# Row means of a 64 MB array: the first load issued as two transfers from two engines

## The chip, the cores and the metric

The kernel runs on one core of a Trainium2 chip. The time is device microseconds of one execution; of three runs of the kernel before, the median is 160.81 us (160.39 to 160.96). The profile is of one execution, taken apart into its engines: DVE (VectorE) and ACT (ScalarE) compute here, POOL (GpSimd) does two small multiplications, SP (SyncE) issues every DMA, and PE (TensorE) does nothing. The data is moved by the core's 16 DMA engines. A DMA is issued by a queue (SP's, in the kernel before), cut into one packet for each of the 128 partitions, and the packets are dealt out to the 16 DMA engines, eight to each.

## The reference

```python
batch, seq, dim = 32, 512, 1024
x = np.random.randn(batch, seq, dim).astype(np.float32)
divisor = float(dim)

def reference(x, divisor):
    return (np.sum(x, axis=-1) / divisor).astype(np.float32)
```

16,384 rows of 1,024 float32 values, 67.1 MB, are read once; 16,384 means, 64 KB, are written.

## The kernel before

The rows are spread over 128 partitions, 128 rows to each. The rows of one load that belong to one partition lie side by side in memory, so a load of n rows is 128 pieces of n x 4 KB. The loads come in this order, by rows per partition: 2 and 14 (list `first`), six of 14 and one of 12 (list `main`), then 9, 4 and 2 (list `last`), and the last row in two halves, `pa` and `pb`. All the loads are issued by SP in program order, one after the other, on one DMA queue (`load`, L182).

The loads of 14 rows, and the first one of 2 rows, go to three buffers in turn (pool `bulk`). So the first three loads (2, 14 and 14 rows) need to wait for nothing. The fourth goes to the buffer of the first, and SP issues it when DVE's reduction of the first load is done; the fifth waits for the reduction of the second, and so on. The tile framework gives each DMA one of eight completion semaphores in turn.

DVE sums most rows with one `reduce_sum` for each load (L205, tile names `res<-t`); from the load numbered eight on, ACT takes some of the rows (L186, `junk<-t`), and for the last 16 rows DVE uses another instruction (L192). POOL multiplies by 1/1024 (L207). Two stores of results are issued by SP during the end of the stream (L223, L224), and the last one, 8 KB, after the last sum (L228).

Three functions rewrite the program after it is built. `start_loads_at_once` takes the DMAs that stand at the head of SP's instructions and wait for nothing (here the first three loads) and puts them ahead of SP's part in the opening barrier, in which all engines meet before the kernel's body. `latest_wait_first` sorts the waits of an instruction that has several. `close_while_storing` puts the last store within the closing barrier. An instruction that has more waits than it can hold gets a small semaphore instruction ahead of it.

Of the kernel before, what the change touches and what calls it, by code (L numbers as in the profile page):

```python
# [13 lines left out]
SP = mybir.EngineType.SP  # L14
DVE = mybir.EngineType.DVE
POOL = mybir.EngineType.Pool


def start_loads_at_once(nc):

    first, body = nc.main_func.blocks[0], nc.main_func.blocks[1]
    loads = []
    for i in body.instructions:
        if i.engine == SP:
            if type(i).__name__ != "InstDMACopy" or (i.sync_info and i.sync_info.on_wait):
                break
            loads.append(i)
    names = {i.name for i in loads}  # L30
    assert names
    body.instructions = [i for i in body.instructions if i.name not in names]
    at = next(
        k for k, i in enumerate(first.instructions) if i.engine == SP and type(i).__name__ == "InstDrain"
    )
    first.instructions = first.instructions[:at] + loads + first.instructions[at:]


def with_sync(i, on_wait=None, on_update=None):
# [29 lines left out]
def close_while_storing(nc, landed):  # L69
# [29 lines left out]
    def first(engine, among):  # L99
        i = next(i for i in among if i.engine == engine)  # L100
        assert type(i).__name__ == "InstDrain"
        return i

    enter, gather = first(SP, rest), first(POOL, rest)
    last = nc.sync.wait_ge(landed, 17).ins
# [20 lines left out]
@with_exitstack  # L126
def kernel(
    ctx: ExitStack,
    tc: tile.TileContext,
    x: bass.AP,  # L130
    divisor: float,
    out: bass.AP,
):
    nc = tc.nc
    landed = nc.alloc_semaphore("landed")
    nc.at_finalize(start_loads_at_once)
    nc.at_finalize(latest_wait_first)
    nc.at_finalize(lambda nc: close_while_storing(nc, landed))
    xf = x.flatten_outer_dims()
    N, D = xf.shape  # L140
    P = nc.NUM_PARTITIONS
    scale = 1.0 / float(divisor)
    J = N // P
    assert J * P == N


    F, L = 16, 16
    M = J - F - L
    W = M + L
    x_first = bass.AP(tensor=x.tensor, offset=0, ap=[[F * D, P], [D, F], [1, D]])  # L150
    x_main = bass.AP(tensor=x.tensor, offset=P * F * D, ap=[[W * D, P], [D, M], [1, D]])
    x_last = bass.AP(tensor=x.tensor, offset=P * F * D + M * D, ap=[[W * D, P], [D, L], [1, D]])
    o_first = bass.AP(tensor=out.tensor, offset=0, ap=[[F, P], [1, F]])
    o_main = bass.AP(tensor=out.tensor, offset=P * F, ap=[[W, P], [1, M]])
    o_last = bass.AP(tensor=out.tensor, offset=P * F + M, ap=[[W, P], [1, L]])


    first = [(2, 0), (14, 0)]
    main = [(14, 0)] * 5 + [(14, 4), (12, 5)]
    last = [(9, 4), (4, 2), (2, 1)]  # L160
    assert sum(n for n, _ in first) == F
    assert sum(n for n, _ in main) == M and sum(n for n, _ in last) == L - 1

    pad = ctx.enter_context(tc.tile_pool(name="pad", bufs=1))
    pad.tile([P, 224], F32, name="pad")
    bulk = ctx.enter_context(tc.tile_pool(name="bulk", bufs=3))
    one = ctx.enter_context(tc.tile_pool(name="one", bufs=1))
    psum = ctx.enter_context(tc.tile_pool(name="junk", bufs=4, space=bass.MemoryType.PSUM))


    c = 512
    t4 = one.tile([P, 4, D], F32, name="t4")
    t2 = one.tile([P, 2, D], F32, name="t2")
    pa = one.tile([P, 768], F32, name="pa")[:, :c]
    pb = one.tile([P, D - c + 16], F32, name="pb")[:, : D - c + 2]
    res0 = one.tile([P, F], F32, name="res0")
    res = one.tile([P, M], F32, name="res")
    fin = one.tile([P, L], F32, name="fin")
    nc.gpsimd.memset(pb[:, D - c :], 0.0)  # L179

    def load(dst, src):
        tc.keep_in_program_order(nc.sync.dma_start(out=dst, in_=src))  # L182

    def act_sum(dst, src, by=1.0):
        junk = psum.tile([P, D], F32, name="junk")
        nc.scalar.activation(junk, src, COPY, scale=by, accum_out=dst)  # L186

    def dve_mean(dst, src, by=scale):


        h = src.shape[-1] // 2
        nc.vector.tensor_tensor_reduce(  # L192
            out=src[:, :h], in0=src[:, :h], in1=src[:, h:], scale=by, scalar=0.0,
            op0=ADD, op1=ADD, accum_out=dst,
        )

    for loads, src, dst in ((first, x_first, res0), (main, x_main, res)):
        j = 0
        for rows, on_act in loads:
            t = bulk.tile([P, 14, D], F32, name="t")  # L200
            load(t[:, :rows, :], src[:, j : j + rows, :])
            d = rows - on_act
            for i in range(d, rows):
                act_sum(dst[:, j + i : j + i + 1], t[:, i, :])
            nc.vector.reduce_sum(out=dst[:, j : j + d], in_=t[:, :d, :], axis=AX)  # L205
            j += rows
        nc.gpsimd.tensor_scalar_mul(out=dst, in0=dst, scalar1=scale)  # L207
    j = 0
    for rows, on_act in last:
        t = bulk.tile([P, 14, D], F32, name="t")[:, :rows, :] if rows > 4 else t4 if rows == 4 else t2  # L210
        load(t, x_last[:, j : j + rows, :])
        d = rows - on_act
        for i in range(rows):
            if i < d:
                dve_mean(fin[:, j + i : j + i + 1], t[:, i, :])
            else:
                act_sum(fin[:, j + i : j + i + 1], t[:, i, :], by=scale)
        j += rows
    load(pa, x_last[:, j, :c])
    load(pb[:, : D - c], x_last[:, j, c:])  # L220


    tc.keep_in_program_order(nc.sync.dma_start(out=o_first, in_=res0))  # L223
    tc.keep_in_program_order(nc.sync.dma_start(out=o_main, in_=res))  # L224

    dve_mean(pb[:, D - c : D - c + 1], pa, by=1.0)
    dve_mean(fin[:, j:], pb)
    tc.keep_in_program_order(nc.sync.dma_start(out=o_last, in_=fin))  # L228
# [35 lines left out]
```

## Time and profile before

| what | value |
|---|---|
| median of three runs | 160.81 us (160.39 to 160.96) |
| span of the profiled execution, first to last instruction | 159.0 us |
| what lies around the span, by the median | 1.81 us |
| DVE busy | 117.2 us (74%) |
| ACT busy | 18.5 us (12%) |
| POOL busy | 1.0 us (1%) |
| DMA packets, bytes | 2448, 67.18 MB |
| rate over the span | 422 GB/s |
| time that packets took, of 16 engines' span | 98.3% |

The page lists no total for the profiled execution other than its span, so what the other runs have beyond it, 1.81 us, is taken as lying around it. Engines that are idle cost nothing unless the chain that ends last goes through them. A DMA packet is put down to the window in which it starts, so a share in a narrow window may be over 1 and in the next under it; wide windows even this out. "SPq" is SP's queue of issues. In a row of the timeline the number before the engine is the duration, and the bracket at the end tells how long the engine was idle and what ended this.

### The profile page before, as it was taken

What the parts mean: (1) busy time and instruction counts of PE and PEld (TensorE: products, weight loads), DVE (VectorE), ACT (ScalarE), POOL (GpSimd) and SP (SyncE); (2) the same over time, 40 slices, a digit from 0 to 9 for tenths busy, and PEclk for the clock granted to TensorE, in tenths of its full rate; (3) what the DMA queues carried; (4) which work ended last, traced back from release to release, by engine and by line L of the source; (5) the groups of instructions that cost most, each with busy time, mean ns of one, the idle gap of its engine ahead of it and who ended that gap; (6) DMA issues with size and microseconds to landing.
All of it is one profiled execution on the core that took longest, in us unless ns stands there. A gap on an engine that the chain in (4) does not pass through costs nothing.

```text
span 159.0 us, 148 instructions
## 1 busy us (share of the span) xinstructions
DVE 117.2 (74%) x29; ACT 18.5 (12%) x33; POOL 1.0 (1%) x7
## 2 busy tenths in 40 slices
DVE  0500059995999599978999599959995996395643
ACT  3000000000000000000000000000000900390684
POOL 0000000000000000000000000000000000001000
DMA  7999999959999999699999999699999999999894
GB/s 278 447 462 462 462 462 462 462 260 433 462 462 462 462 462 462 303 390 462 462 462 462 462 462 404 303 447 462 462 462 429 396 396 408 482 445 445 350 420 169
DMA packets 2448, 67.18 MB, mean 422 GB/s; under 512 B 656, under 2 KB 656, under 8 KB 912
## 3 DMA queue, kind: packets, MB, share of 16 engines
q1 hardware_dynamic: 2448, 67.18, 98.3%
HBM read 67.11 MB, written 0.07 MB: 422 GB/s over the span
## 4 chain that ended last, share of the span: by engine, by line
DMA 77%; DVE 21%; SPq 1%; issue 0%; DVEq 0%
DMA t<-in_x_dram 56%; DMA pb<-in_x_dram 21%; DVE res L205 20%; SPq L182 1%; DVE pb L192 0%; DVEq L259 0%
## 5 line engine op out<-in xcount | busy, mean ns | idle before, releaser
L205 DVE TENSOR_REDUCE res<-t 128x14 f32<-128x14336 f32 (+3 forms) x9 | 111.2, 12360 | 34.0 <-DMA t<-in_x_dram 34.0
L186 ACT ACTIVATE junk<-t 128x1024 f32<-128x1024 f32 x16 | 16.2, 1013 | 136.8 <-DMA t<-in_x_dram 136.8
L192 DVE CUSTOM_DVE_ANT_0 t<-t 128x512 f32<-128x512 f32 x8 | 5.1, 688 | 6.1 <-DMA t<-in_x_dram 6.1
L186 ACT ACTIVATION_READ_ACCUMULATOR junk<-t 128x1 f32 x16 | 3.0, 186 | 0.0
L207 POOL TENSOR_SCALAR res<-res 128x16 f32<-128x16 f32 (+1 forms) x2 | 0.7, 352 | 143.3 <-DVE res L205 143.3
L186 ACT ACT_TABLE_LOAD x1 | 1.3, 1283 | 1.7 <-PEq L245 1.7
L192 DVE DVE_READ_ACCUMULATOR2_ANT fin<- 128x1 f32 x9 | 0.7, 82 | 0.0
L192 DVE CUSTOM_DVE_ANT_0 pb<-pb 128x257 f32<-128x257 f32 x1 | 0.4, 428 | 0.2 <-DMA pb<-in_x_dram 0.2
L192 DVE CUSTOM_DVE_ANT_0 pa<-pa 128x256 f32<-128x256 f32 x1 | 0.4, 426 | 0.0
L179 POOL MEMSET pb<- 128x2 f32 x1 | 0.1, 99 | 1.3 <-POOLq L245 1.3
L245 POOL MEMSET const-bfloat16-1.0<- 128x1 bf16 x1 | 0.1, 101 | 0.0
L245 POOL MEMSET const-uint8-127<- 128x1 uint8 x1 | 0.1, 101 | 0.0
L245 POOL MEMSET const-float32-0.0<- 128x1 f32 x1 | 0.1, 98 | 0.2 <-issue 0.2
L245 POOL MEMSET const-float32-1.0<- 128x1 f32 x1 | 0.1, 98 | 0.0
L192 DVE DVE_READ_ACCUMULATOR2_ANT pb<- 128x1 f32 x1 | 0.1, 84 | 0.0
## 6 DMA issues: line engine op xcount, KB each, us to landing
t<-in_x_dram SPq DMA_DIRECT2D x7, 7168.0 KB, 35.6
t<-in_x_dram SPq DMA_DIRECT2D x1, 6144.0 KB, 33.3
t<-in_x_dram SPq DMA_DIRECT2D x1, 4608.0 KB, 27.2
t<-in_x_dram SPq DMA_DIRECT2D x2, 1024.0 KB, 19.2
t<-in_x_dram SPq DMA_DIRECT2D x1, 2048.0 KB, 31.7
pa<-in_x_dram SPq DMA_DIRECT2D x1, 256.0 KB, 33.8
pb<-in_x_dram SPq DMA_DIRECT2D x1, 256.0 KB, 33.9
out_dram<-res SPq DMA_DIRECT2D x1, 48.0 KB, 11.6
```

The costliest lines, as they stand in the source:

```text
L179: nc.gpsimd.memset(pb[:, D - c :], 0.0)
L182: tc.keep_in_program_order(nc.sync.dma_start(out=dst, in_=src))
L186: nc.scalar.activation(junk, src, COPY, scale=by, accum_out=dst)
L192: nc.vector.tensor_tensor_reduce(out=src[:, :h], in0=src[:, :h], in1=src[:, h:], scale=by, scalar=0.0, op0=ADD, op1=ADD, accum_out=dst,)
L205: nc.vector.reduce_sum(out=dst[:, j : j + d], in_=t[:, :d, :], axis=AX)
L207: nc.gpsimd.tensor_scalar_mul(out=dst, in0=dst, scalar1=scale)
L245: nc = _bacc.Bacc("TRN2", target_bir_lowering=False, num_devices=1)
```

## The change

The first load of two rows per partition becomes two DMAs of one row per partition. SP issues the first row, ACT the second. The function that moves loads ahead of the opening barrier does so now for SP and for ACT. The buffer, the computation, and every other load are as they were. The first reduction on DVE, and the load that later takes the buffer, each wait for both DMAs. Completion semaphores are handed out in turn, so each later load has the next one of the eight.

```diff
-    loads = []
-    for i in body.instructions:
-        if i.engine == SP:
-            if type(i).__name__ != "InstDMACopy" or (i.sync_info and i.sync_info.on_wait):
-                break
-            loads.append(i)
-    names = {i.name for i in loads}
-    assert names
-    body.instructions = [i for i in body.instructions if i.name not in names]
-    at = next(
-        k for k, i in enumerate(first.instructions) if i.engine == SP and type(i).__name__ == "InstDrain"
-    )
-    first.instructions = first.instructions[:at] + loads + first.instructions[at:]
+    for engine in (SP, ACT):
+        loads = []
+        for i in body.instructions:
+            if i.engine == engine:
+                if type(i).__name__ != "InstDMACopy" or (i.sync_info and i.sync_info.on_wait):
+                    break
+                loads.append(i)
+        names = {i.name for i in loads}
+        assert names
+        body.instructions = [i for i in body.instructions if i.name not in names]
+        at = next(
+            k
+            for k, i in enumerate(first.instructions)
+            if i.engine == engine and type(i).__name__ == "InstDrain"
+        )
+        first.instructions = first.instructions[:at] + loads + first.instructions[at:]
...
             t = bulk.tile([P, 14, D], F32, name="t")
-            load(t[:, :rows, :], src[:, j : j + rows, :])
+            if rows == 2:
+                load(t[:, 0, :], src[:, 0, :])
+                tc.keep_in_program_order(nc.scalar.dma_start(out=t[:, 1, :], in_=src[:, 1, :]))
+            else:
+                load(t[:, :rows, :], src[:, j : j + rows, :])
```

The two-row load in the list `last` is made by other lines and stays one DMA.

## The prediction, made before the changed kernel ran

> **What bounds the kernel now.** I read the table of windows first, for when the DMA engines are idle; then the chain that ended last, for what stands at its ends; then the timeline around the first loads, for the slack between the transfers and DVE; last, the end.
>
> The windows (columns: from, to, length, busy time of DVE, ACT and POOL with instruction counts, PE clock, DMA share, GB/s):
>
> ```profile
> 0.00:1.00 1.00, 0.00 (x0) 0.00 (x0) 0.19 (x4) 1.00 0.00 0
> 1.00:2.00 1.00, 0.00 (x0) 0.26 (x1) 0.10 (x1) 1.00 0.95 197
> 2.00:4.00 2.00, 0.00 (x0) 1.02 (x1) 0.00 (x0) 1.00 1.07 455
> 4.00:21.00 17.00, 2.29 (x1) 0.00 (x0) 0.00 (x0) 1.00 1.00 435
> 21.00:123.00 102.00, 90.52 (x6) 0.00 (x0) 0.26 (x1) 1.00 1.01 438
> ...
> 155.00:157.00 2.00, 1.07 (x4) 1.70 (x4) 0.00 (x0) 1.00 0.93 336
> 157.00:159.00 2.00, 0.43 (x2) 0.01 (x1) 0.00 (x0) 1.00 0.05 4
> ```
>
> Nothing moves in the first microsecond; in the second the engines are occupied (0.95) but at less than half the later rate; from 2 us on the share is about 1 until 155. So the kernel is one stream of 67.1 MB on 16 DMA engines that never run dry, with a start of about 2 us and a tail of about 2 us. DVE is busy 90.52 of 102 us in the middle, so it waits for the stream and not the stream for it.
>
> The chain that ended last, in order of time:
>
> ```profile
> 0.00 4.61 DMA t<-in_x_dram
> 4.61 0.02 issue
> 4.63 2.30 DVE res L205
> 6.93 0.02 issue
> 6.95 48.45 DMA t<-in_x_dram
> ```
>
> It goes through the first load, the first reduction and the fourth load's issue. That looks as if the first load's landing were on the path. It is not: the 48.45 us from 6.95 are mostly the fourth load standing in the queue behind loads two and three, as the timeline shows:
>
> ```profile
> 4.63 2.29 DVE L205 TENSOR_REDUCE res<-t 128x2 f32<-128x2048 f32 x1 [4.63 <-DMA t<-in_x_dram]
> 21.51 15.09 DVE L205 TENSOR_REDUCE res<-t 128x14 f32<-128x14336 f32 x1 [14.59 <-DMA t<-in_x_dram]
> 38.44 15.09 DVE L205 TENSOR_REDUCE res<-t 128x14 f32<-128x14336 f32 x1 [1.84 <-DMA t<-in_x_dram]
> 55.42 15.09 DVE L205 TENSOR_REDUCE res<-t 128x14 f32<-128x14336 f32 x1 [1.89 <-DMA t<-in_x_dram]
> ```
>
> Loads of 14 rows land at 21.5, 38.4 and 55.4, 16.93 to 16.98 us apart; DVE needs 15.09 for one and idles 1.8 to 1.9 before each. The fourth load, issued at 6.95, is first served when the third is nearly in, about 38. Its issue has some 30 us to spare. After the first reduction DVE idles 14.59 us.
>
> The end, from the timeline:
>
> ```profile
> 153.37 1.03 ACT L186 ACTIVATE junk<-t 128x1024 f32<-128x1024 f32 x1 [0.61 <-DMA t<-in_x_dram]
> 155.86 1.03 ACT L186 ACTIVATE junk<-t 128x1024 f32<-128x1024 f32 x1 [0.30 <-DMA t<-in_x_dram]
> 157.10 0.43 DVE L192 CUSTOM_DVE_ANT_0 pb<-pb 128x257 f32<-128x257 f32 x1 [0.17 <-DMA pb<-in_x_dram]
> 157.56 0.33 SPq L228 DMA_DIRECT2D out_dram<-fin  x1
> ```
>
> The last half row lands, DVE adds it, the last store is issued, and 1.4 us later it has landed. The end moves only if the stream ends earlier or later.
>
> **The change, part by part.** The sum is made on the profiled span, 159.0; the 1.81 us between it and the median is kept as it is, since no row shows it.
>
> SP's first issue. It covers the same 128 partitions with pieces of 4 KB instead of 8. SP's issue rows are 0.33 to 0.48 us long, whether a packet has 57 KB or 64 bytes, so halving bytes doesn't shorten it (the first one's row is 0.38). Loads two and three follow at 0.43 and 0.91 as before. Cost 0.
>
> ACT's issue. By the trace, ACT reaches its drain in the opening barrier at 0.13 us, SP at 1.40 behind its three issues, and the barrier opens at about 1.67. One issue of up to 0.48 brings ACT there at about 0.6: hidden behind SP's. If ACT needed over 1.4 us, the barrier would open later; behind it are ACT's table load (1.28 us, needed at 123.1), the small memset (needed at the end) and SP's wait for the first reduction. Cost 0 in either case; the DMAs themselves are ahead of it.
>
> The stream. The same bytes, in one DMA more. Two rows price a DMA of its own. A load of seven megabytes takes 16.93 us (21.51 to 38.44), one of a single megabyte takes 2.49 (153.37 to 155.86). With f for what a DMA costs beside its bytes and m for a megabyte: f+7m=16.93, f+m=2.49, so m=2.41 and f=0.08. The packet records, finer than the 10 ns of those rows, give less: packets of 2, 8, 16 and 56 KB follow one another on an engine every 80, 306, 607 and 2113 ns, which is 4.8 ns per packet and 36.8 per KB (1,000 bytes); eight packets and a 6 ns completion more per engine make 0.044 us. I take 0.06, between the two; ends 0.04 and 0.08. All of it is on the path, since the stream never pauses.
>
> Here a page of the Trainium skill speaks against the change. "DMA: Bandwidth & Descriptors", section "Anatomy of one DMA", fits a DMA as 2.0 us and its bytes over 436 GB/s, and the page's rules ask for at least 1 MiB in each; the first load would now be two of half that. If those 2 us were paid in the stream, the sum would be 162.8. The rows above price a further DMA behind others at 0.08 (the fit is for GpSimd's path, and its 2 us are mostly a completion that others can overlap), so I go by the rows.
>
> The start. By the packet records the 16 engines start their first packet between 1.02 and 1.68 us (1.21 in the mean), and it takes 745 ns in the mean, 1,006 at most, where a later 8 KB one takes 309. Whenever an engine started, its first data is in at about 2.0: the wait is for a common start, not for a queue that was too slow. What a second queue does to this, the trace of before can't show; only one queue is in it. Bound from below: if all late starts (1.21-1.02=0.19) and all of the slow first packet (745-309=0.44) went, -0.63. Bound from above, if the second queue pays a slow first packet of its own behind the first's: +0.44. I take 0, since the engines end their first packets together at 2.0 however early they began, and ACT's issue is 0.1 us later than SP's and can't bring that forward.
>
> Order within the stream. Two queues now feed each engine. In the best order the eight packets of ACT's row alternate with the eight of SP's and the load is in at 4.7. In the worst, ACT's come late and each waits for a packet of 56 KB of load two: eight times 2.11 us, so it is in at about 21.5. Then the first reduction ends at 23.8, the second runs 23.8 to 38.9 instead of 21.5 to 36.6, the third starts 0.45 us late and ends at 54.0, and the fourth starts on time at 55.42. The fourth load is issued at 23.8, still 14 us before it can be served. Cost 0 in both; what hides it is the queue of two loads, and if it were late beyond 37 each further microsecond would empty the stream by one.
>
> Further waits. DVE's first reduction and SP's fourth issue wait for two semaphores, so a 17 ns semaphore row each, in front of slack of 14 us. The last store waits for ACT and a DMA that has long landed; POOL's chain of closing waits has the same number of members and ends 0.9 us before the last store. Cost 0.
>
> The sum: 159.0+0.06=159.06 for the span, and with 1.81 it is 160.87, so 160.9.
>
> **Rivals.** First, slower: taking turns between two queues costs the engines something at each change. For it: each queue's first access here costs 0.44 us more than a later one, and no row shows two queues at work, so a change may cost a part of that. Against it: between two DMAs of one queue an engine loses 6 ns. Each engine has eight packets of the second queue; if every one pays the whole 0.44, it is 8x0.44=3.5 and the time 164.4; it decides (0.8 us) from 0.10 us per turn on. At 0.15 it gives 162.1.
>
> Second, a faster start: requests of two queues overlap and the slow first packet goes. For it: 0.95 share at 197 GB/s in the second microsecond. Against: it needs first data before 2.0 us. At most 160.87-0.63=160.2, which still can't be told from no change; more would need a shorter first microsecond, and there SP's issue is unchanged.
>
> Third, the two issues get in each other's way, as if one came behind the other: the first packets come one issue later, 0.38 to 0.43 us, and the stream with them: 161.3. For it: both are issued within 0.13 us of each other. Against: SP issues its second load 0.43 after its first, when the first's packets aren't yet moving, so issuing and moving overlap.
>
> That the change does nothing, as the first load isn't what the stream waits for, is the forecast itself.
>
> **How the numbers follow.** A difference of 0.5%, 0.8 us, is about what a measurement of this kernel can tell from no change (the three runs span 0.57). The stream as it is: 0.53, from 160.4 to 161.4 with the runs' spread. Turns that cost over 0.10 us: 0.25, 161.7 to 164.4, mostly under 162.2. A faster start: 0.14, about half of it beyond my bound through something in the 1.8 us that no row shows. Issues in each other's way: 0.08. Faster by over 0.5% is then 0.07, slower 0.25, and within 0.68. The range 160.1 to 162.1 leaves out the 0.07 below and some 0.12 above.
>
> **What would show it.** DMA packets 2448+128+16=2592 over two queues in the table of queues, same bytes; an issue on ACT's queue near 0.1 us; the first reduction starting at 4.7 (or as late as 21.5, harmless); loads two to four landing at 21.6, 38.5 and 55.5, each 0.06 later; the same share of 1 from 2 us on; the last half row at 157.2. If turns cost, the second load lands late, beyond 22.3, and all later landings by as much. A faster start shows as all landings early by one amount. I am wrong if the landings of loads four and later move by more than 0.8 us, or if the time moves while the span doesn't.

## The result, and the profile after

The changed kernel takes 161.28 us (median of six runs, 161.21 to 161.31), the one before 160.84 in the same session (six runs, 160.39 to 160.96). The ratio is 1.0037, with a 95% interval of 1.0022 to 1.0052: slower by about 0.44 us, clear of noise, and within the 0.5% set as the bound. The forecast was 160.9, in a range of 160.1 to 162.1. The six runs of the kernel before stand in two groups here, two at 160.4 and four at 160.8 to 161.0. In the three later sessions its median is 160.46 to 160.50; against that the change would cost 0.8 us, 0.5%.

The table of windows of the changed kernel, with the columns of the one before (from, to, length, busy time of DVE, ACT and POOL, PE clock, DMA share, GB/s):

```profile
0.00:1.00 1.00, 0.00 (x0) 0.00 (x0) 0.19 (x4) 1.00 0.02 4
1.00:2.00 1.00, 0.00 (x0) 0.28 (x1) 0.10 (x1) 1.00 0.84 193
2.00:4.00 2.00, 0.00 (x0) 1.01 (x1) 0.00 (x0) 1.00 0.98 330
4.00:21.00 17.00, 2.29 (x1) 0.00 (x0) 0.00 (x0) 1.00 1.03 443
21.00:123.00 102.00, 90.52 (x6) 0.00 (x0) 0.26 (x1) 1.00 1.01 436
```

The second microsecond is as it was (193 GB/s, 197 before). From 2 to 4 us the DMA engines are almost fully occupied (0.98, before 1.07) and move 330 GB/s where they moved 455. (One packet of 56 KB that starts just before 4 us is counted whole in the 455; by the time in flight, from the packet records, it is 335 against 419.) Later the rate is the same again. A share near 1 with a low rate means packets that take longer, not an idle queue.

The timeline of DVE, the first four reductions:

```profile
5.61 2.29 DVE L213 TENSOR_REDUCE res<-t 128x2 f32<-128x2048 f32 x1 [5.61 <-DMA t<-in_x_dram]
22.53 15.09 DVE L213 TENSOR_REDUCE res<-t 128x14 f32<-128x14336 f32 x1 [14.63 <-DMA t<-in_x_dram]
39.48 15.09 DVE L213 TENSOR_REDUCE res<-t 128x14 f32<-128x14336 f32 x1 [1.86 <-DMA t<-in_x_dram]
56.38 15.09 DVE L213 TENSOR_REDUCE res<-t 128x14 f32<-128x14336 f32 x1 [1.81 <-DMA t<-in_x_dram]
```

Against 4.63, 21.51, 38.44 and 55.42 before, the landings are later by 0.98, 1.02, 1.04 and 0.96. The loss is there when the first load has landed, and nothing is added or given back. The end, from the timeline:

```profile
158.00 0.43 DVE L196 CUSTOM_DVE_ANT_0 pb<-pb 128x257 f32<-128x257 f32 x1 [0.19 <-DMA pb<-in_x_dram]
158.47 0.33 SPq L236 DMA_DIRECT2D out_dram<-fin  x1
```

The last half row is 0.90 later than before (157.10), and so is the end: the span is 159.9 against 159.0. The table of queues shows the change as described, 144 packets on a second queue:

```profile
q1 hardware_dynamic: 2448, 66.65, 96.9%
q10 hardware_dynamic: 144, 0.52, 1.0%
```

Why 0.90 between the profiles and 0.44 between the medians? In every run here the time is 1.3 to 1.4 us above the span (the profiled run of the changed kernel: 161.24 and 159.90, so 1.34). The profiled execution of before, with its 159.0, thus took about 160.34, and was among the quickest of its kernel, whose runs in all sessions have spans from 159.0 to 159.6. The six runs of the changed kernel have 159.9 to 160.0.

The packet records of the two traces (not shown in a view) tell where the first load lost its time. Its 128 packets of 8 KB took 309 ns each once the first were through, at 2.5 us, without exception. Of the 167 packets of 4 KB that start after 2.5 us in the changed kernel, 38 are stretched by more than 20 ns over the usual 159, between 3.0 and 4.2 us, on either queue, to as much as 455. That is 0.34 us for each engine in the mean; eight more packets and short waits make up the rest of the mean engine's delay. But the loss isn't spread evenly: the second load lands on the 16 engines between 21.12 and 21.49 before (21.38 in the mean), between 21.45 and 22.51 after (21.83). The mean engine is 0.45 late, the last one 1.02, and a load is complete with its last engine. The end follows the last one. In the twelve other traces that can be compared with that of before (the changed kernel's and eleven of the experiments'), the last engine's landing of load four and the span are later than before by amounts that agree within 0.12 us, up to 2.4 us. The mean over the engines doesn't do this: with the split as the second load it is 0.29 late at load four, the last engine 0.74, and the span 0.65.

### The profile page after: what moved, and what is told of

It reads as the page before. It is cut to its first block, busy times and chain, and to the rows that moved or that the text cites. A ratio compares the mean times of both kernels' runs of the same rounds, so it can differ in the third digit from the quotient of the medians.

```text
span 159.9 us, 150 instructions
## 1 busy us (share of the span) xinstructions
DVE 117.2 (73%) x29; ACT 18.5 (12%) x33; POOL 1.0 (1%) x7
## 4 chain that ended last, share of the span: by engine, by line
DMA 77%; DVE 21%; SPq 1%; issue 0%; DVEq 0%
DMA t<-in_x_dram 56%; DMA pb<-in_x_dram 21%; DVE res L213 20%; SPq L186 1%; DVE pb L196 0%; DVEq L267 0%
```

## The experiments

Each ran three rounds or more beside the kernel before, in three sessions of four; before took 160.46 us in the first session, 160.50 in the second (from the four DMAs of 2 KB on) and 160.48 in the third (from the one DMA of small pieces on). A ratio is always to before in the same session, with its 95% interval. The first question was whether the loss belongs to the second queue (called Q in the expectations) or to the split (P).

**Both rows from SP.** The function that moves the loads is that of before; ACT issues nothing.

```diff
-                tc.keep_in_program_order(nc.scalar.dma_start(out=t[:, 1, :], in_=src[:, 1, :]))
+                load(t[:, 1, :], src[:, 1, :])
```

> Both one-row loads are issued by SP, one after the other, ahead of the barrier; ACT issues nothing. Theory Q (the loss comes from the second queue): no packet of 4 KB is stretched after 3 us, the first reduction starts at about 4.7, loads two and three land 16.9 us apart as before, and the span is 159.0 to 159.5, 0.06 above what the kernel before has in the same state. Theory P (pieces of 4 KB and one DMA more, whatever the queue): the same as the changed kernel, first reduction at about 5.6, span about 159.9.

160.92 us, 1.0031 (1.0019 to 1.0043). The windows and the first reductions:

```profile
1.00:2.00 1.00, 0.00 (x0) 0.00 (x0) 0.00 (x0) 1.00 0.88 127
2.00:4.00 2.00, 0.00 (x0) 1.28 (x1) 0.10 (x1) 1.00 0.99 338
...
5.57 2.29 DVE L209 TENSOR_REDUCE res<-t 128x2 f32<-128x2048 f32 x1 [5.57 <-DMA t<-in_x_dram]
22.40 15.09 DVE L209 TENSOR_REDUCE res<-t 128x14 f32<-128x14336 f32 x1 [14.55 <-DMA t<-in_x_dram]
```

One queue, no turns between queues, no issue by ACT, and nearly the same loss: 338 GB/s, first reduction at 5.57. The split costs about this wherever it is issued from. Q isn't needed for the loss. But the loss doesn't lie in quite the same place. Here the second microsecond is already poorer (127 GB/s, 193 in the changed kernel), and by the packet records about half of what the mean engine loses beyond the kernel before is lost by 2.5 us: 0.95 us by then, where the kernel before and the changed one have lost 0.70 and 0.71.

**The whole first load from ACT.** One DMA of 8 KB pieces again, on ACT's queue.

```diff
-                load(t[:, 0, :], src[:, 0, :])
-                tc.keep_in_program_order(nc.scalar.dma_start(out=t[:, 1, :], in_=src[:, 1, :]))
+                tc.keep_in_program_order(nc.scalar.dma_start(out=t[:, :2, :], in_=src[:, :2, :]))
```

> The two-row load is one DMA of 8 KB pieces again, but issued by ACT; SP issues loads two and three ahead of the barrier. Theory Q: a stall of some 0.4 us in the mean and up to 1 us for the slowest engine while both queues are served; landings of loads two and later about 1 us later than before, span about 159.9. Theory P: no stall, span 159.0 to 159.5. In both, if the engines take turns by packets, the first load now alternates with packets of 56 KB and lands between 15 and 21.5 us, and the end is not moved by that, since the fourth load is only needed at 37.

160.70 us, 1.0015 (1.0005 to 1.0024), span 159.4: between the two. DVE's timeline:

```profile
22.17 17.28 DVE L212 TENSOR_REDUCE res<-t 128x2 f32<-128x2048 f32 x2 [22.17 <-DMA t<-in_x_dram]
```

The first reduction starts at 22.17, 17.5 us later than before (the row has the first two, back to back), and the time is 0.24 us above before. So the landing of the first load isn't what the end follows; its packets had taken turns with the 56 KB ones, one for one.

**SP's next loads behind the barrier; ACT's issue behind the barrier.** Two variants of the changed kernel. In the first, only one load of each engine is moved ahead of the barrier:

```diff
+        loads = loads[:1]
         names = {i.name for i in loads}
```

In the second, only SP's loads are:

```diff
-    for engine in (SP, ACT):
+    for engine in (SP,):
```

> As the changed kernel, but SP's second and third load stay behind the opening barrier, so that SP issues one DMA before it and not three. If ACT's descriptors came late (first packet at 2.44 us) because three issues of SP were ahead of them, ACT's first packet now comes at 1.1 to 1.6, and if the stall belongs to that crowding it goes: span 159.0 to 159.5. If ACT's queue is late by itself, its first packet stays at about 2.4 and the stall and the span of 159.9 stay.

> As the changed kernel, but ACT's issue stays behind the opening barrier, at about 1.7 us. Theory Q: the stall comes with the second queue, now about 1.6 us later, amid load two's packets of 56 KB; the landings of loads three and later are about as late as in the changed kernel, span 159.9. If the stall needs the start-up (small packets of both queues together), it goes and the span is 159.0 to 159.5. The first load, alternating with 56 KB packets, lands between 10 and 21.5 us without any effect on the end.

161.12 us, 1.0042 (1.0027 to 1.0057), with ACT's first packet at 2.61; and 161.24 us, 1.0056 (1.0039 to 1.0072), with spans of 159.7 and 159.9. SP's issues aren't what makes ACT's packets late: they came 2.3 us after the issue in the changed kernel, 2.5 with a single issue of SP ahead of them, where SP's first come after 1.0. With ACT's issue late, at 1.74, its packets first move at 5.4 between the 56 KB ones, the first load lands at 24.5, and the loss is the same or more; it then lies before 3 us, in SP's own eight packets for each engine. One window and the first reductions with ACT's issue late (the last row has the first two, back to back):

```profile
1.00:2.00 1.00, 0.00 (x0) 0.00 (x0) 0.10 (x1) 1.00 0.93 115
...
24.48 17.28 DVE L213 TENSOR_REDUCE res<-t 128x2 f32<-128x2048 f32 x2 [24.48 <-DMA t<-in_x_dram]
```

Holding either back mends nothing. And with ACT's issue late, the loss is there before the packets of the second DMA of the split move at all, while SP's queue has as many DMAs as in the kernel before, only with a first one of half the size.

**Four DMAs of 2 KB pieces, from SP, or from both engines.** From SP, the function that moves the loads is that of before. The second pair of theories was that descriptors are made as they are used at a limited rate (G), or that each DMA more costs a fixed time at the start (C).

```diff
-                load(t[:, 0, :], src[:, 0, :])
-                tc.keep_in_program_order(nc.scalar.dma_start(out=t[:, 1, :], in_=src[:, 1, :]))
+                for r in range(2):
+                    for h in (0, 512):
+                        load(t[:, r, h : h + 512], src[:, r, h : h + 512])
```

> The two-row load as four DMAs of 2 KB pieces, all issued by SP. Theory G (at the start the descriptors are made while they are used, some 1.4 us for each DMA's 128 pieces, the distance between SP's first packet at 1.0 and ACT's at 2.4; pieces that move faster than that starve the engines): the last of four sets is made at 1.0+4x1.4=6.6, the first reduction starts at 6.8 to 7.3, span 161.2 to 161.8. Theory C (each DMA more at the start costs a fixed 0.45 us, as both rows from SP did): three more, 1.35, span 160.3 to 160.5. The forecast's price of 0.06 per DMA: span 159.2.

For the other one, SP issues the two halves of the first row and ACT those of the second:

```diff
-                load(t[:, 0, :], src[:, 0, :])
-                tc.keep_in_program_order(nc.scalar.dma_start(out=t[:, 1, :], in_=src[:, 1, :]))
+                for h in (0, 512):
+                    load(t[:, 0, h : h + 512], src[:, 0, h : h + 512])
+                    tc.keep_in_program_order(
+                        nc.scalar.dma_start(out=t[:, 1, h : h + 512], in_=src[:, 1, h : h + 512])
+                    )
```

> The same four DMAs of 2 KB pieces, two issued by SP and two by ACT, all ahead of the barrier. Theory G with one source of descriptors for both queues: as with all four on SP, first reduction at 6.8 to 7.3, span 161.2 to 161.8. Theory G with a source for each queue: two sets each, made by 3.8, first reduction at about 4.8 and span 159.1 to 159.5. Theory C: span 160.3 to 160.5.

From SP alone: 162.78 us, 1.0146 (1.0129 to 1.0164). From both: 160.74 us, 1.0012 (1.0002 to 1.0021). The windows and first reductions, from SP alone,

```profile
2.00:4.00 2.00, 0.00 (x0) 0.86 (x1) 0.10 (x1) 1.00 1.00 310
...
7.16 2.29 DVE L210 TENSOR_REDUCE res<-t 128x2 f32<-128x2048 f32 x1 [7.16 <-DMA t<-in_x_dram]
23.99 15.09 DVE L210 TENSOR_REDUCE res<-t 128x14 f32<-128x14336 f32 x1 [14.54 <-DMA t<-in_x_dram]
```

and from both:

```profile
2.00:4.00 2.00, 0.00 (x0) 1.28 (x1) 0.10 (x1) 1.00 1.02 387
...
5.33 2.29 DVE L216 TENSOR_REDUCE res<-t 128x2 f32<-128x2048 f32 x1 [5.33 <-DMA t<-in_x_dram]
22.04 15.09 DVE L216 TENSOR_REDUCE res<-t 128x14 f32<-128x14336 f32 x1 [14.43 <-DMA t<-in_x_dram]
```

Four DMAs on one queue cost 2.3 us, as G had it (7.16 in its 6.8 to 7.3), and not three times 0.45. By the packet records the first two of the four flow freely until about 2.7 us; of the packets of the third and fourth many are stretched, to nearly 1 us, and some engines stand idle between them. It looks as if the supply of descriptors ran out there. The same four on two queues show no stretched packet after 2.5 us and cost 0.24, so what is short would be short for each queue, not for both together. The changed kernel, with one DMA of the split on each queue and yet stretched packets, doesn't fit that.

**The split where it is served late.** The kernel before, in which the other two-row load, near the end, is split in the same way.

```diff
-        load(t, x_last[:, j : j + rows, :])
+        if rows == 2:
+            load(t[:, 0, :], x_last[:, j, :])
+            load(t[:, 1, :], x_last[:, j + 1, :])
+        else:
+            load(t, x_last[:, j : j + rows, :])
```

> The first load stays one DMA of 8 KB pieces, as in the kernel before; the other two-row load, near the end of the stream, becomes two DMAs of 4 KB pieces, both issued by SP at about 122 us, 30 us before they are served. Theory G: the descriptors are there long before, so no packet is stretched and the end moves by the 0.04 to 0.08 us forecast: not to be told from before. Theory C, or any cost of 4 KB pieces by themselves: the last half row lands 0.4 us later or more, time 0.3% above before.

160.53 us, 1.0004 (0.9994 to 1.0013): not to be told from before. All 256 packets take 159 ns. The end of the timeline:

```profile
153.50 1.03 ACT L186 ACTIVATE junk<-t 128x1024 f32<-128x1024 f32 x1 [0.60 <-DMA t<-in_x_dram]
155.99 1.03 ACT L186 ACTIVATE junk<-t 128x1024 f32<-128x1024 f32 x1 [0.31 <-DMA t<-in_x_dram]
```

The split megabyte takes 2.49 us, as the whole one did (153.37 to 155.86).

**Halves by partitions.** The two issuers of the change, but each with 64 partitions of 8 KB pieces.

```diff
-                load(t[:, 0, :], src[:, 0, :])
-                tc.keep_in_program_order(nc.scalar.dma_start(out=t[:, 1, :], in_=src[:, 1, :]))
+                load(t[:64, :2, :], src[:64, :2, :])
+                tc.keep_in_program_order(nc.scalar.dma_start(out=t[64:, :2, :], in_=src[64:, :2, :]))
```

> The two-row load as two DMAs issued at once by SP and ACT, as in the changed kernel, but cut by partitions and not by rows: 64 pieces of 8 KB each, 128 in all as before. Theory G: as many pieces as before, each as large as before, so the engines don't starve: first reduction at 4.6 to 4.9, span 159.0 to 159.4. Theory C, or a loss that belongs to the second queue: span 159.5 to 159.9, first reduction after 5.0.

162.82 us, 1.0143 (1.0126 to 1.0159), spans of 161.5: 2.3 us slower, against every theory. Its only profiled execution took 186.0 us, its 56 KB packets 2.44 us each where they take 2.12 in the kernel before; so no line of it is shown. But its packet records have ACT's 64 packets at 0.52 to 0.66 us each, with all 16 engines at work, and the 8 KB packets late in the same execution at 0.35. So a DMA to 64 partitions moved its bytes there at little over half the usual rate; for the eight packets of each engine that is up to 2.2 us more, about what the four other runs lost. Why half the partitions get half the rate, no run here tests.

**One DMA with the same small pieces.** The kernel before, with the two rows going to rows 0 and 2 of the buffer, so that one DMA has 256 pieces of 4 KB.

```diff
-            load(t[:, :rows, :], src[:, j : j + rows, :])
+            rows_of_t = slice(0, 3, 2) if rows == 2 else slice(0, rows)
+            load(t[:, rows_of_t, :], src[:, j : j + rows, :])
...
-            nc.vector.reduce_sum(out=dst[:, j : j + d], in_=t[:, :d, :], axis=AX)
+            summed = t[:, rows_of_t, :] if rows == 2 else t[:, :d, :]
+            nc.vector.reduce_sum(out=dst[:, j : j + d], in_=summed, axis=AX)
```

> The two-row load is one DMA issued by SP, but its rows go to rows 0 and 2 of the buffer, so it has 256 pieces of 4 KB and not 128 of 8 KB. If the loss goes with small pieces at the start, it is there as with two DMAs: the first reduction starts at 5.2 or later, span 159.5 to 160.0, time 0.4 to 0.5 us above before. If it goes with the number of DMAs, one DMA costs only its eight further packets for each engine (0.04 us): first reduction at 4.7, span 159.0 to 159.3, time as before.

160.57 us, 1.0009 (1.0000 to 1.0019).

```profile
2.00:4.00 2.00, 0.00 (x0) 1.10 (x1) 0.00 (x0) 1.00 1.01 416
...
5.03 2.29 DVE L207 TENSOR_REDUCE res<-t 128x2 f32<-128x2048 f32 x1 [5.03 <-DMA t<-in_x_dram]
21.91 15.09 DVE L207 TENSOR_REDUCE res<-t 128x14 f32<-128x14336 f32 x1 [14.60 <-DMA t<-in_x_dram]
```

416 GB/s and not 338, and none of its packets after 2.5 us is stretched. (In the mean the engines are in at 4.58; the last makes it 5.0.) This is the same data in the same pieces on the same queue as with both rows from SP; only the number of DMAs is one and not two. G in its plain form, so much time for 128 pieces, fell here: 256 pieces of one DMA come fast enough.

**Two DMAs of larger pieces.** The change with a first load of four rows, two from each engine (and a second of twelve).

```diff
-    first = [(2, 0), (14, 0)]
+    first = [(4, 0), (12, 0)]
...
-            if rows == 2:
-                load(t[:, 0, :], src[:, 0, :])
-                tc.keep_in_program_order(nc.scalar.dma_start(out=t[:, 1, :], in_=src[:, 1, :]))
+            if rows == 4:
+                load(t[:, :2, :], src[:, :2, :])
+                tc.keep_in_program_order(nc.scalar.dma_start(out=t[:, 2:4, :], in_=src[:, 2:4, :]))
```

> The first load has four rows per partition (the second twelve); SP and ACT issue two rows each, at once, ahead of the barrier. Two DMAs on two queues as in the changed kernel, but of 8 KB pieces. If the loss goes with pieces that are moved faster than they are supplied, pieces of twice the size hide it: landing of the third load as before (38.4 to 38.6), span 159.0 to 159.4. If it goes with the second DMA or the second queue: span 159.5 to 159.9.

160.73 us, 1.0017 (1.0008 to 1.0026), span 159.4, the third load in at 39.0. By the packet records hardly a packet is stretched after 2.5 us, so 8 KB pieces do hide the later stretch. But the first packets of SP's DMA are in between 1.95 and 2.6 us, where before they are in between 1.5 and 2.1; the mean engine has lost 1.05 us by 3 us, where before it is 0.70. So a loss remains, in the first packets, and neither expectation holds whole: less than with 4 KB pieces, more than nothing.

**The split as the second load; a whole first load of four rows.** Both on the kernel before. In the first, the two rows come second and are two DMAs of SP:

```diff
-    first = [(2, 0), (14, 0)]
+    first = [(14, 0), (2, 0)]
...
-            load(t[:, :rows, :], src[:, j : j + rows, :])
+            if rows == 2:
+                load(t[:, 0, :], src[:, j, :])
+                load(t[:, 1, :], src[:, j + 1, :])
+            else:
+                load(t[:, :rows, :], src[:, j : j + rows, :])
```

In the second, no load is split:

```diff
-    first = [(2, 0), (14, 0)]
+    first = [(4, 0), (12, 0)]
```

> The load of fourteen rows comes first, and behind it on SP's queue the two-row load as two DMAs of one row each. Same addresses, same 4 KB pieces, same two DMAs as with both rows from SP, only served at about 18 us and not at 1. If the loss belongs to the start, all 256 of these packets take about 159 ns; if it belongs to these addresses (rows 64 KB apart) or to any such split, many are stretched to 200 to 400 again. The time also has what it costs to begin with pieces of 56 KB, which this doesn't separate: 160.5 to 160.9.

> The kernel before with a first load of four rows (one DMA of 16 KB pieces by SP) and a second of twelve. If smaller pieces at the start lose more, larger ones might lose less than the 0.70 us that the kernel before loses in its first microsecond: time 0.1 to 0.3 us below before. If that loss is the wait for the first data and has nothing to do with the pieces, the time is that of before within 0.1 us; if large first pieces spread the engines further apart, 0.1 to 0.3 above.

The first took 161.07 us, 1.0034 (1.0022 to 1.0046); at about 18 us, 229 of the 256 packets take 159 ns and 18 are stretched by more than 20 ns, to 286 at most. So the addresses are not to blame for the changed kernel's 455, though a few stretched ones are left. Why the whole is 0.59 us above before isn't separated: it begins with 56 KB pieces, and it has the few stretched packets. The second took 160.47, 1.0001 (0.9992 to 1.0010): larger first pieces bring nothing. No variant beat the kernel before.

## Why the prediction was right or wrong

**What bounds the kernel**: right, and shown. The stream sets the time; a shift of the stream in its first microseconds is at the end unchanged (0.98 at the first landing, 0.90 at the last half row).

**SP's and ACT's issues, the waits, the order within the stream**: right. ACT issues at 0.12, its drain follows at 0.54, and SP's is still the last before the barrier. The two queues alternate packet by packet. The slack was tested beyond what the change needs: a first reduction at 22.17 moved the time by no more than 0.24 us. The extra DMA's price, 0.06, fits where its packets are served late: 0.03, within -0.10 to 0.21, near the end of the stream. The 2.0 us for a DMA that the Trainium skill gives in "DMA: Bandwidth & Descriptors", section "Anatomy of one DMA", were not paid there, as the prediction had expected.

**The start**: this is the term that was mis-sized. It was put at 0, between -0.63 and +0.44, on the ground that first data is in at 2.0 however early an engine began. That held: by 2.5 us the engines have lost as much as before (0.71 against 0.70 in the mean). What the step left out is the time after, 2.5 to 4.4 us, when the second DMA's packets are served fresh from their issue. It costs 0.40 to 0.45 in the mean, close to the upper end and for another reason than the one given for it; and the last engine, which is the one that counts, loses 1.0 of profile against profile. The step reasoned with means over the engines, while a load is in with its last engine. Between medians the whole is 0.44 where 0.06 was forecast. That it stayed within 0.5% is in part luck: against the 160.48 that the kernel before takes in the last session, 161.28 is at 0.5%, and two variants of the change lost 0.66 and 0.78 us.

**The prediction's own signs.** Its landings were to be 0.06 later, and it called itself wrong if those of loads four and later moved by more than 0.8 us. Load four moved by 0.96 between the two profiles (55.42 to 56.38). About 0.47 of this is that the profiled execution of before was quicker than the median; but the sign was given for the profile, and by it the start was priced wrong. The measurement, too, could tell 0.37% from no change, where the prediction had put its limit at about 0.5%.

**Rivals.** Turns that cost: on the right side, and their sign was met (the second load beyond 22.3, at 22.53, and the later ones as late), but not the mechanism. In the changed kernel a packet of either queue starts 155 ns after one of the other when nothing else disturbs them, and the loss is as large with one queue. A faster start: not seen. Issues in each other's way, the first packets one issue later: SP's first packet comes at 1.00, as before. ACT's come 1.4 us after SP's, which none of the rivals had.

**The sum's frame.** The 1.81 us said to lie around the span were about 1.34 around it, and 0.47 by which the profiled execution was quicker than the median.

**What is shown, and what stays open.** Shown: in the changed kernel the loss lies in packets stretched between 3.0 and 4.2 us; the split pays about as much from one queue as from two; one DMA of the same pieces doesn't pay it, nor does the same split served late; four DMAs on the one queue take it to 2.3 us. So at the start one DMA is cheaper than several for the same bytes. Why is not shown. That the loss goes with the number of DMAs that a queue is to serve while they have only just been issued fits these runs, but not the one with ACT's issue behind the barrier: there SP's queue has as many DMAs as before, and the loss is there before ACT's packets move, though ACT's issue, at 1.74, falls amid it. That a first DMA of half the size loses by itself, whatever comes after it, fits that run, but not the four DMAs on two queues (0.24 us), and no run tests it alone. Open as well: what in the supply is limited, if it is supply; why four DMAs on two queues pay less than two on two queues (0.44, in another session); and why some engines pay more than twice the mean.

## What to carry to other kernels

Where the stream is the bound, begin it with one DMA and not with several. A split that cost 0.46 us at the start cost nothing that could be measured late in the queue; and neither smaller pieces in one DMA (0.09 us) nor larger ones (0.01 us less) changed much. Price a startup by the last of the 16 engines, not by their mean. Before adding a profiled span to what lies around it, look where in the spread of the runs that execution stands.

## What the runs showed of the hardware that was not expected

- A further DMA at the start of the stream costs far more than one in its midst, and more than in proportion: from SP, two DMAs for one megabyte cost 0.46 us, four (of 2 KB pieces) 2.3, where near the end two cost 0.03.
- The four issued by two engines cost 0.24 instead of 2.3 us.
- With an issue of SP 0.12 us ahead of it, ACT's first packet came 2.0 (2 KB pieces) to 2.5 us after its issue, and 3.6 us after it where SP's pieces were of 56 KB; SP's came after 1.0.
- Two queues alternate packet by packet with pieces of 4 and 8 KB; with pieces of 2 KB, by the records, mostly eight of one DMA and then eight of the other.
- Two DMAs of 64 partitions each took 2.3 us more than one of 128 for the same megabyte, with packets of 0.52 to 0.66 us where 8 KB ones otherwise took 0.35 in that execution.
